# A new written-out order for the attention layer, and the second layer's gate summed by VectorE and DMA instead of TensorE

## The chip, the cores and the metric

One core of a Trainium2 chip runs the whole program. The metric is device time in microseconds (us) of one execution. The names of engines are those of the profile: PE is TensorE (PEld its weight loads), DVE is VectorE, ACT is ScalarE, POOL is GpSimd, SP is SyncE, which issues the big loads. Times inside the profiled execution are counted from its first instruction.

## The reference

A decoder trunk of two layers over 256 tokens of width 1024, batch 1, all in float32. Cut to what matters:

```python
for i in range(2):
    shift, scale, gate = split(c @ ada_w[i] + ada_b[i], 3)      # each of width 1024
    h = rmsnorm(x, norm_g[i]) * (1 + scale) + shift
    y = nsa_mixer(h, ...) if i == 0 else mlstm_mixer(h, ...)
    x = x + gate * y
return rmsnorm(x, final_g)
```

Layer 0 is sparse attention with three branches: keys and values compressed by a small network (`gelu(flat @ w1 + b1) @ w2 + b2`), selected blocks, and a sliding window. With 256 tokens the last two see all keys that the causal mask leaves. Layer 1 is a chunkwise mLSTM with 8 heads. Both multiply the mixer's output by a SiLU gate path and project it with `w_out`. The `gate` of each layer is a product of the vector `c` (1024) with a 1024x1024 part of `ada_w`.

## The kernel before

**Numbers.** A weight arrives as a float32 tile (`raw`, 128x1024, 512 KB). ACT rounds it into `wh` (L169, the step `hi`), DVE writes the rest into `wl` (L174, `lo`), and every product is three matmuls: `wh` with the high part of the activations, `wl` with it, `wh` with the low part. There are 10 `raw` buffers and 6 pairs of `wh` and `wl`.

**The loads.** One list of loads is issued by SP in its order (L86). A load is issued when the buffer that it takes over is free, so SP stands still behind a load that has no buffer.

**Layer 0** (`first_phase`, `nsa`, `attention`) runs under a manual schedule: each engine executes its instructions exactly as the program writes them. `first_phase` multiplies the first weights as they arrive. From then on the string `ORDER` sets the order of all engines and of the loads. Its words are steps:

- `k:kk,part` multiplies part of the key and value weights of one 128-row block; `hi` and `lo` make the next weight's halves. A `hi` also appends the next weight to the list of loads.
- `hidden:n` (L584) multiplies two loads of the compressing network's first weight, four in all. `gelu:0..2` (L669 to L676) is its activation, spread over DVE, ACT (`Square` L670, `Tanh` L674) and DVE (L676). `turned` (L681) is the first matmul behind it.
- `S:n,a` scores, `m` minima, `e` exponentials, `f` factors, `T` transposes on PE (L830), `t` their copies, for eight pairs of heads `n` and two halves of the tokens.
- `sXY:n,j` scales the probabilities by the factors (L825), branch 0 on engine X and branch 1 on engine Y, where p, v and a stand for POOL, DVE and ACT. Each letter is two instructions, called a pair here.
- `z:n,q` are steps of the gate path's products (twelve matmuls 128x256 each), `d` columns of layer 1's scale and shift (DVE, L873).
- `gp:k` loads one block of layer 0's gate weight and scales it by `c` on ACT (L652). `ga:k` adds it to the tile `gate0` with an adding DMA that POOL issues (L889). Before it POOL copies one column of `gate0` (L888, `seen`), which waits until the adding DMA before has landed. POOL executes in order, so all that stands behind `seen` waits too.

**Layer 1** (`layer2`) is ordered by the framework's scheduler, engine by engine. Loops run over 8 heads (`head`), four pairs of wide products (`og_unit`, `z_post`) and 16 blocks of the output weight (`project`, `finish`). Its gate (`gate_sums`, twice, for 512 columns each) multiplies the gate weights by `c` in eight DVE instructions (L1050), splits the sum into two float32r parts (ACT L1053, DVE L1054), sums over partitions with two matmuls against ones (L1057), which also spread the sum over all partitions, and copies the result into `gate1` (ACT, L1058). POOL multiplies a quarter of each output weight by `gate1` (L165). The half with columns 512 to 1023 comes first.

Of the kernel before, what the change touches and what calls it, by code (L numbers as in the profile page):

```python
# [23 lines left out]
class Kernel:  # L24
# [605 lines left out]
    ckeys cscores:1 cscores:0 ccopy:1 cvalues:0 sap:1,0 T:1,0,1 t:1,0,1 S:2,0 spp:1,1 d:0,2 S:2,1 zo:0 T:0,1,1 gp:4 cvalues:1 lo d:0,3 T:0,1,0 t:0,1,1  # L630
    m:2,0 m:2,1 z:1,0 ccopy:0 ctokens:0 t:0,1,0 cdist:0 ctokens:1 cdist:1 e:2,0 e:2,1 T:1,0,0 t:1,0,0 z:1,1 d:1,0 T:1,1,1 t:1,1,1 S:3,0 hi z:1,2 gp:5
    S:3,1 T:1,1,0 lo t:1,1,0 f:2 cexp m:3,0 V:0 V:1 cprobs ga:4 spp:2,0 T:2,0,0 m:3,1 z:1,3 e:3,0 T:2,0,1 S:4,0 hi cparts:0 S:4,1 t:2,0,0 cparts:1
    zt:1 spv:2,1 zo:1 t:2,0,1 cturned:0 lo e:3,1 f:3 T:2,1,0 T:2,1,1 t:2,1,0 ga:5 t:2,1,1 z:2,0 z:2,1 m:4,0 m:4,1 S:5,0 cpt:0 e:4,0 z:2,2 sap:3,0
    T:3,0,1 T:3,0,0 spv:3,1 C:0 z:2,3 d:1,1 e:4,1 d:1,2 t:3,0,1 t:3,0,0 S:5,1 f:4 y:0 T:3,1,1 lo hi gp:6 T:3,1,0 t:3,1,0 m:5,0 svp:4,0 V:2 t:3,1,1 V:3
    T:4,0,0 ga:6 spa:4,1 m:5,1 T:4,0,1 S:6,0 zt:2 e:5,0 e:5,1 t:4,0,1 t:4,0,0 cturned:1 lo S:6,1 zo:2 z:3,0 d:1,3 d:2,0 T:4,1,1 C:1 T:4,1,0 f:5 hi
    z:3,1 z:3,2 hi t:4,1,1 m:6,0 y:1 gp:7 spv:5,0 T:5,0,1 t:4,1,0 m:6,1 d:2,1 e:6,0 svp:5,1 t:5,0,1 lo z:3,3 cpt:1 Y:0 T:5,0,0 lo t:5,0,0 e:6,1 f:6
    V:4 T:5,1,1 ga:7 T:5,1,0 S:7,0 C:2 t:5,1,0 m:7,0 t:5,1,1 spa:6,1 zt:3 S:7,1 m:7,1 zo:3 spa:6,0 d:2,2 d:2,3 d:3,0 V:5 out:0 d:3,1 T:6,0,1 e:7,1
    e:7,0 f:7 gs T:6,1,0 gc g4 Y:1 t:6,0,1 out:1 t:6,1,0 T:6,0,0 T:6,1,1 params d:3,2 l:1,1,2 l:0,1,2 l:1,0,2 y:2 hi hi t:6,1,1 t:6,0,0 lo saa:7,1
    T:7,1,0 sap:7,0 T:7,0,1 t:7,0,1 t:7,1,0 l:0,0,2 l:0,1,3 hi T:7,1,1 t:7,1,1 T:7,0,0 t:7,0,0 d:3,3 lo lo Y:2 hi nh:0 hi lo V:6 V:7 C:3 l:0,0,3 y:3
    l:0,0,4 nl:0 l:0,1,4 l:0,1,5 l:0,0,5 Y:3 l:0,0,6 lo nh:3 nl:3 l:0,0,7 l:0,1,6 l:0,1,7 root l:1,1,3 l:1,0,3 l:1,1,4 g5 r:0,0 l:1,0,4 l:1,0,5 sq:0,0  # L640
    l:1,0,6 r:0,1 nh:2 sq:0,1 nl:2 sc:0 x:0,1 nh:1 x:0,0 l:1,0,7 tr:0,0 nh:4 nl:1 rp:1,0 tr:0,1 md:0,1 l:1,1,5 md:0,0 ro:0,0 re:0,0 l:1,1,6 ro:0,1
# [605 lines left out]
    def layer2(self):  # L1247
        nc, t, pc, p2, ident = self.nc, self.t, self.pc, self.p2, self.ident
        pcb = self.pcb
        g = nc.gpsimd  # L1250
# [300 lines left out]
        self.gate1 = self.T(pc, [P, D], tag="gate")  # L1551
        ones = self.T(p2, [P, P], F32R)
        bias = self.T(p2, [P, D])
        g.memset(ones.bitcast(F32), 1.0)
        g.memset(bias, 0.0)
        nc.gpsimd.dma_start(bias[0:1], t["ada_b"][1:2, 2048:3072])
# [113 lines left out]
```

## Time and profile before

| what | value |
|---|---|
| time of three runs | 419.70, 420.06, 420.30 us; median 420.06 |
| time of the profiled execution | 419.18 us |
| its span, first to last instruction | 417.4 us |
| PE busy | 406.9 us (97%) |
| DVE, ACT, POOL busy | 342.8, 282.8, 93.7 us |
| granted TensorE clock, mean | 0.998 of full speed |

The difference between the profiled time and its span, 1.8 us, lies around the program. A busy PE is not PE without loss: matmuls overlap, so a short wait shows in the distance between their starts rather than in the busy time.

### The profile page before, as it was taken

The numbers are of one execution on the slowest core, as the hardware profiler recorded it, in microseconds if no ns is written. First come the engines' busy times: TensorE is split into PE (matmuls) and PEld (weight loads), VectorE is DVE, ScalarE is ACT, GpSimd is POOL, SyncE is SP. The second block draws the span as 40 slices with busy tenths as digits, with TensorE's granted clock in tenths as the row PEclk, the third lists the DMA queues.
The fourth block names the chain that finished last, engine by engine and source line by source line (L and its number), as shares of the span: only waits on it lengthen the run. The fifth ranks groups of instructions, "written<-read, shape, count | busy, mean of one in ns | idle before, by whom it ended". The sixth has DMA issues, their size and how long they took to land.

```text
span 417.4 us, 7543 instructions
## 1 busy us (share of the span) xinstructions
PE 406.9 (97%) x2641; PEld 356.5 (85%) x2641; DVE 342.8 (82%) x716; ACT 282.8 (68%) x558; POOL 93.7 (22%) x163
## 2 busy tenths in 40 slices
PE   8999999989999999999999999999999999999994
PEld 5899998679889788888998999888888888888884
DVE  6999898979999999878782798899859996557553
ACT  6766687899999997767549866557446554564523
POOL 4000132256664420152324100000001241320000
PEclk9999999999999999999999999999999999999999
DMA  8999999999788988258684676378455776630002
GB/s 318 409 408 406 400 378 367 323 360 365 214 265 267 337 287 316 87 164 292 218 302 156 204 216 233 110 251 254 149 199 203 233 254 219 195 108 2 0 1 102
DMA packets 28616, 99.89 MB, mean 239 GB/s; under 512 B 3685, under 2 KB 3793, under 8 KB 28449
## 3 DMA queue, kind: packets, MB, share of 16 engines
q1 hardware_dynamic: 26208, 92.30, 62.3%
q0 software_dynamic: 2224, 6.83, 6.9%
q8 instruction: 21, 0.34, 0.3%
q10 hardware_dynamic: 144, 0.26, 0.2%
q14 instruction: 19, 0.15, 0.1%
HBM read 94.61 MB, written 1.10 MB: 229 GB/s over the span
## 4 chain that ended last, share of the span: by engine, by line
PE 90%; DMA 5%; ACT 2%; DVE 1%; SPq 1%; issue 0%; DVEq 0%; ACTq 0%
PE bank L549 10%; PE bank L550 10%; PE bank L551 10%; PE bank L439 8%; PE bank L1586 6%; PE bank L1584 6%; PE bank L1585 6%; PE bank L912 5%; PE bank L1497 5%; PE bank L1068 5%; PE bank L1179 4%; PE bank L847 3%; PE bank L830 3%; DMA raw<-in_start 2%; DMA raw<-in_path 2%; PE bank L1377 2%
## 5 line engine op out<-in xcount | busy, mean ns | idle before, releaser
L174 DVE TENSOR_TENSOR wl<-raw,wh 128x1024 fp32r<-128x1024 f32 (+4 forms) x119 | 138.2, 1175 | 36.1 <-ACT wh L169 35.2
L169 ACT ACTIVATE wh<-raw 128x1024 fp32r<-128x1024 f32 (+4 forms) x119 | 118.2, 1008 | 70.6 <-PE bank L551 31.8
L549 PE MATMUL bank<-wh,one 128*128 128x512 f32 (+2 forms) x208 | 77.1, 371 | 0.0
L550 PE MATMUL bank<-wl,one 128*128 128x512 f32 (+2 forms) x208 | 76.4, 367 | 0.0
L551 PE MATMUL bank<-wh,one 128*128 128x512 f32 (+2 forms) x208 | 76.2, 367 | 0.0
L1584 PE MATMUL bank<-one,wh 128*128 128x256 f32 x208 | 59.6, 286 | 0.0
L1586 PE MATMUL bank<-one,wl 128*128 128x256 f32 x208 | 59.0, 284 | 0.1
L1585 PE MATMUL bank<-one,wh 128*128 128x256 f32 x208 | 58.9, 283 | 0.0
L549 PEld LDWEIGHTS bank<-wh,one 128*128 128x128 f32 x208 | 39.2, 189 | 6.6 <-issue 0.4
L551 PEld LDWEIGHTS bank<-wh,one 128*128 128x128 f32 x208 | 39.2, 189 | 6.2
L550 PEld LDWEIGHTS bank<-wl,one 128*128 128x128 f32 x208 | 39.3, 189 | 5.9
L1586 PEld LDWEIGHTS bank<-one,wl 128*128 128x128 f32 x208 | 39.8, 192 | 0.3 <-DVE wl L174 0.3
L1584 PEld LDWEIGHTS bank<-one,wh 128*128 128x128 f32 x208 | 39.8, 192 | 0.2
L1585 PEld LDWEIGHTS bank<-one,wh 128*128 128x128 f32 x208 | 39.9, 192 | 0.2
L825 POOL TENSOR_SCALAR Pr<-Pr,f 128x128 f32<-128x128 f32 (+1 forms) x34 | 31.3, 941 | 27.1 <-DVE f L816 14.4
L439 PE MATMUL bank<-one,wh 128*128 128x256 f32 x224 | 29.8, 284 | 0.6 <-ACT one L413 0.4
L439 PEld LDWEIGHTS bank<-one,wh 128*128 128x128 f32 x224 | 28.1, 192 | 1.1 <-ACT one L413 0.6
L808 ACT ACTIVATE Pr<-Pr,mn 128x128 f32<-128x128 f32 (+1 forms) x64 | 28.2, 451 | 0.0
L165 POOL TENSOR_TENSOR raw<-raw,gate 128x256 f32<-128x256 f32 x16 | 16.4, 1035 | 47.0 <-DMA raw<-in_out_b 23.7
L1358 DVE SCALAR_TENSOR_TENSOR conv<-bank,one,conv 128x255 f32<-128x255 f32 (+2 forms) x48 | 20.1, 470 | 2.2 <-ACT conv L1353 2.2
L873 DVE CUSTOM_DVE_ANT_0 raw<-raw,one,one 128x1024 f32<-128x1024 f32 x16 | 20.6, 1311 | 0.0
L801 DVE CUSTOM_DVE_ANT_0 Pr<-bank,one 128x128 f32<-128x128 f32 (+1 forms) x64 | 18.7, 352 | 0.0
(343 smaller groups left out, 807.9 us busy)
## 6 DMA issues: line engine op xcount, KB each, us to landing
raw<-in_wide SPq DMA_DIRECT2D x44, 512.0 KB, 4.3
raw<-in_units SPq DMA_DIRECT2D x18, 512.0 KB, 4.7
raw<-in_turn SPq DMA_DIRECT2D x16, 512.0 KB, 6.1
raw<-in_out_b SPq DMA_DIRECT2D x16, 512.0 KB, 4.0
raw<-in_start SPq DMA_DIRECT2D x8, 512.0 KB, 9.8
Q<-in_columns SPq DMA_DIRECT2D x8, 512.0 KB, 9.6
raw<-in_gate SPq DMA_DIRECT2D x8, 512.0 KB, 7.8
raw<-in_path SPq DMA_DIRECT2D x8, 512.0 KB, 8.5
```

The source lines that it names most:

```text
L169: self.nc.scalar.activation(v(hi), src, AF.Copy)
L174: (g or self.nc.vector).tensor_tensor(v(lo), src, v(hi).bitcast(F32), op=OP.subtract)
L439: nc.tensor.matmul(out, w[:, ch * P : ch * P + P], h[:, kk], start=(kk == 0 and m == 0 and ch % 2 == 0), stop=(kk == 7 and m == 2), skip_g ...
L549: nc.tensor.matmul(out, self.hh[:, kk, sl], wh, start=first, stop=False, skip_group_check=True)
L550: nc.tensor.matmul(out, self.hh[:, kk, sl], wl, start=False, stop=False, skip_group_check=True)
L551: nc.tensor.matmul(out, self.hl[:, kk, sl], wh, start=False, stop=last, skip_group_check=True)
L808: nc.scalar.activation(v, v, AF.Exp, bias=mn[:, a, br, j : j + 1], scale=-1.0, accum_out=sm[:, a, br, j : j + 1])
L825: es[br].tensor_scalar(v, v, f, None, op0=OP.mult)
L912: nc.tensor.matmul(out, l[:, sl], w[:, c0:c1], start=(k == 0 and m == 0), stop=(k == 7 and m == 2), skip_group_check=True)
L1584: nc.tensor.matmul(out, wh, self.hh[:, kk], start=first, stop=False, skip_group_check=skip)
L1585: nc.tensor.matmul(out, wh, self.hl[:, kk], start=False, stop=False, skip_group_check=skip)
L1586: nc.tensor.matmul(out, wl, self.hh[:, kk], start=False, stop=last, skip_group_check=skip)
```

## The change

Two things. The string `ORDER` is written anew as a whole, with the same steps but for the engines of some scalings; the loads follow it. In the second layer `gate_sums` no longer uses PE: DVE transposes the 128x512 sum in 32x32 blocks, sums the 32 values of each row, transposes again, and the four quarters of the partitions are joined over scratch in DRAM (`quarters`, then `whole`), read back as `four`, summed once more by DVE, and spread over 128 partitions by a DMA. Four DMAs of a half are issued by POOL and pinned in program order; each waits for the one ahead. The half of columns 512 to 1023 is now written ahead of head 4, the other one ahead of the third pair of wide products, and the eight loads of the gate weights move up in the list by one pair each.

```diff
     ORDER = """
-    hi k:0,0 k:0,1 hi lo lo hi k:0,2 k:1,0 lo gp:0 ga:0 k:1,2 k:2,0 k:1,1 hi k:2,2 k:3,0 k:4,0 qa:3 lo d:0,0 E:0,0 k:2,1 k:3,1 E:1,0 hi lo E:1,1 k:3,2
...
+    gp:0 hi lo k:0,0 k:0,1 k:0,2 hi k:1,0 k:1,1 k:1,2 k:2,2 lo k:3,2 hi hi lo k:4,2 hi lo lo k:2,1 E:1,0 k:3,1 k:2,0 k:4,1 E:0,0 hi lo k:5,2 k:6,2
...
         for n in range(4):
-            if n >= 2:
-                self.gate_stream(3 - n)
+            if n in (1, 2):
+                self.gate_stream(2 - n)
             pair(3 + n)
...
-    def gate_sums(self, n, bias, ones, out, bi):
+    def gate_sums(self, n, bias, out):
...
-        parts = [self.T(self.p2, [P, 512], F32R, tag="conv", bufs=2) for _ in range(2)]
-        nc.scalar.activation(parts[0], acc, AF.Copy)
-        nc.vector.tensor_sub(parts[1], acc, parts[0].bitcast(F32))
-        bank = self.bank(bi)
-        for m, w in enumerate(parts):
-            nc.tensor.matmul(bank, ones, w, start=(m == 0), stop=(m == 1))
-        nc.scalar.activation(out[:, 512 * n : 512 * n + 512], bank, AF.Copy)
+        turned = self.T(p2, [P, 512], tag="conv", bufs=2)
+        nc.vector.transpose(turned, acc)
+        sums, rows = [self.T(p2, [P, 32]) for _ in range(2)]
+        g.memset(sums, 0.0)
+        nc.vector.tensor_reduce(sums[:, 0:16], turned.rearrange("p (j r) -> p j r", r=32), axis=AX.X, op=OP.add)
+        nc.vector.transpose(rows, sums)
+        pin = self.tc.keep_in_program_order
+        parts = self.pd.tile([P, 32], F32, name=self.nm("quarters"), tag="quarters%d" % n)
+        whole = self.pd.tile([16, 32], F32, name=self.nm("whole"), tag="half%d" % n)
+        four, one = self.T(p2, [16, 4, 32]), self.T(p2, [16, 32])
+        pin(g.dma_start(parts, rows))
+        pin(g.dma_start(four, parts.rearrange("(i j) c -> j i c", i=4)[0:16]))
+        nc.vector.tensor_reduce(one, four.rearrange("j i c -> j c i"), axis=AX.X, op=OP.add)
+        pin(g.dma_start(whole, one))
+        pin(g.dma_start(out[:, 512 * n : 512 * n + 512], whole.rearrange("j c -> (j c)").unsqueeze(0).partition_broadcast(P)))
...
         for n in range(2):
+            if n:
+                self.gate_sums(1, bias, self.gate1)
             head(4 * n)
...
         for n in range(2, 4):
-            self.gate_sums(3 - n, bias, ones, self.gate1, 6)
+            if n == 2:
+                self.gate_sums(0, bias, self.gate1)
             bs = wide_bs()
```

The loads that SP issues around the four `hidden` steps, before (`in_hidden` are the compressing network's weights, `in_gate` layer 0's gate weight, `in_path` the gate path's, `in_turn` columns):

```order
L86 DMA raw_734<-in_path 128x1024
L86 DMA raw_784<-in_hidden 128x1024
L86 DMA raw_837<-in_hidden 128x1024
...
L86 DMA raw_935<-in_gate 128x1024
L86 DMA raw_958<-in_path 128x1024
L86 DMA raw_961<-in_path 128x1024
L86 DMA raw_1018<-in_hidden 128x1024
L86 DMA raw_1020<-in_hidden 128x1024
L86 DMA raw_1033<-in_turn 128x1024
```

And the same places of SP's list now:

```order
L86 DMA raw_734<-in_hidden 128x1024
L86 DMA raw_784<-in_hidden 128x1024
...
L86 DMA raw_902<-in_gate 128x1024
L86 DMA raw_905<-in_path 128x1024
L86 DMA raw_939<-in_hidden 128x1024
L86 DMA raw_996<-in_hidden 128x1024
L86 DMA raw_1006<-in_hidden 128x1024
L86 DMA raw_1008<-in_hidden 128x1024
L86 DMA raw_1030<-in_path 128x1024
```

The last two `in_hidden` loads, which `hidden:3` reads, stand one place further up, and the `in_path` loads are spread among the others.

ACT between the first exponentials and the `Tanh` of the compressing network (L674), before (`raw_1062` is a load of the gate path's weight, `one_160` a copy of values, `raw_1035` a block of the gate weight):

```order
L808 ACTIVATE Pr_1105,sm_1076<-Pr_1105,mn_1075 128x256 x2
L808 ACTIVATE Pr_1106,sm_1076<-Pr_1106,mn_1075 128x256 x2
L670 ACTIVATE y_228_1135<-y_227_1134 128x256
L652 ACTIVATE raw_1035<-raw_1035,one_8_72 128x1024
L169 ACTIVATE wh_1162<-raw_1062 128x1024
L619 ACTIVATE one_160_810<-bank_826 128x512
L674 ACTIVATE y_228_1135<-y_228_1135 128x256
```

And now:

```order
L169 ACTIVATE wh_1103<-raw_1030 128x1024
L808 ACTIVATE Pr_1106,sm_1090<-Pr_1106,mn_1089 128x128 x2
L808 ACTIVATE Pr_1107,sm_1090<-Pr_1107,mn_1089 128x128 x2
L670 ACTIVATE y_223_1117<-y_222_1116 128x256
L808 ACTIVATE Pr_1106,sm_1090<-Pr_1106,mn_1089 128x256 x2
L808 ACTIVATE Pr_1107,sm_1090<-Pr_1107,mn_1089 128x256 x2
L674 ACTIVATE y_223_1117<-y_223_1117 128x256
L652 ACTIVATE raw_1071<-raw_1071,one_8_72 128x1024
```

No load stands between the two functions any more: the weight `wh` is made ahead of the exponentials, and the gate's block behind `Tanh`.

POOL at the first scalings (L825), before; L888 is the copy that waits for the adding DMA before, L889 the next adding DMA, and L698 to L312 are memsets:

```order
L825 TENSOR_SCALAR Pr_1105<-Pr_1105,f_1145 128x128
L825 TENSOR_SCALAR Pr_1105<-Pr_1105,f_1145 128x256
L825 TENSOR_SCALAR Pr_1106<-Pr_1106,f_1145 128x128
L825 TENSOR_SCALAR Pr_1106<-Pr_1106,f_1145 128x256
L698 MEMSET one_251_1275 128x128
L699 MEMSET y_252_1276 128x256
L311 MEMSET one_25_103 128x8
L312 MEMSET one_27_104 128x8
L888 COPY seen_1309<-gate_813 128x1
L889 DMA gate_813<-raw_1035 128x1024
```

And now:

```order
L825 TENSOR_SCALAR Pr_1106<-Pr_1106,f_1163 128x128
L825 TENSOR_SCALAR Pr_1106<-Pr_1106,f_1163 128x256
L888 COPY seen_1225<-gate_813 128x1
L889 DMA gate_813<-raw_1071 128x1024
L698 MEMSET one_251_1257 128x128
L699 MEMSET y_252_1258 128x256
L311 MEMSET one_25_103 128x8
L312 MEMSET one_27_104 128x8
L825 TENSOR_SCALAR Pr_1107<-Pr_1107,f_1163 128x128
L825 TENSOR_SCALAR Pr_1107<-Pr_1107,f_1163 128x256
...
L825 TENSOR_SCALAR Pr_1189<-Pr_1189,f_1341 128x128
```

Half of the first pair of heads (`Pr_1107`, both branches) is now scaled by POOL alone, behind an adding DMA. In the whole layer POOL has 19 pairs of scalings where it had 17, and three halves more (0,1, 3,1 and 4,1) whose two branches are both its own.

## Rows read from the trace of the kernel before

**Rows 1.** The page: busy time of each engine, with its share of the span and its instructions.

```profile
PE 406.9 (97%) x2641; PEld 356.5 (85%) x2641; DVE 342.8 (82%) x716; ACT 282.8 (68%) x558; POOL 93.7 (22%) x163
```

**Rows 2.** Stretches of the span: us, busy time of each engine (with instructions), granted clock, busy share of the DMA engines, GB/s.

```profile
core 0: us, PE busy (x) PEld busy (x) DVE busy (x) ACT busy (x) POOL busy (x), PEclk, DMA share, GB/s
66.00:71.00 5.00, 5.00 (x44) 4.18 (x44) 3.67 (x5) 4.36 (x7) 1.11 (x2) 1.00 1.04 397
71.00:78.00 7.00, 6.18 (x44) 3.46 (x42) 6.44 (x22) 6.97 (x18) 3.29 (x6) 1.00 1.02 312
78.00:87.00 9.00, 7.73 (x60) 6.60 (x57) 6.07 (x23) 6.51 (x18) 4.01 (x9) 1.00 1.03 320
...
100.00:120.00 20.00, 20.00 (x168) 18.27 (x167) 19.59 (x68) 19.42 (x61) 9.42 (x14) 1.00 0.84 262
120.00:140.00 20.00, 20.00 (x174) 17.24 (x173) 19.86 (x75) 19.68 (x61) 12.43 (x15) 1.00 0.90 262
```

**Rows 3.** The timeline of PE from 68 to 87 us: start, length, engine, line, operation, tiles, count, and in brackets idle time ahead of it and what ended it.

```profile
68.98 5.40 PE L584 MATMUL bank<-raw,Pr 128*64 128x256 f32 x48
...
74.90 0.40 PE L782 MATMUL bank<-KH,Q 128*128 128x512 f32 x1
...
75.69 0.50 PE L782 MATMUL bank<-KH,Q 128*128 128x512 f32 x1 [0.15 <-DVE Q L578]
...
76.44 0.65 PE L584 MATMUL bank<-raw,Pr 128*64 128x256 f32 x2
...
77.73 1.94 PE L584 MATMUL bank<-raw,Pr 128*64 128x256 f32 x14 [0.65 <-DMA raw<-in_hidden]
...
79.61 0.38 PE L549 MATMUL bank<-wh,one 128*128 128x256 f32 x1
...
84.69 0.49 PE L830 MATMUL bank<-one,Pr 128*128 128x128 f32 x3
86.45 0.41 PE L681 MATMUL bank<-one,y 128*128 128x128 f32 x2 [1.27 <-DVE y L676]
```

**Rows 4.** The timelines of ACT and DVE just ahead of that last wait.

```profile
84.00 1.06 ACT L169 ACTIVATE wh<-raw 128x1024 fp32r<-128x1024 f32 x1 [2.02 <-DMA raw<-in_path]
...
85.44 0.41 ACT L674 ACTIVATE y<-y 128x256 f32<-128x256 f32 x1
...
85.88 0.43 DVE L676 SCALAR_TENSOR_TENSOR y<-y,y 128x256 f32<-128x256 f32 x1 [2.41 <-ACT y L674]
```

**Rows 5.** Loads and adding DMAs: the timelines of SP and POOL, SP's own waits (us in total, times, longest), an issue group (KB each, us to landing), and the landing times of the seven adding DMAs (L889).

```profile
64.81 1.46 SPq L86 DMA_DIRECT2D raw<-in_path  x2
70.95 1.50 SPq L86 DMA_DIRECT2D raw<-in_hidden  x2
74.41 5.30 SPq L86 DMA_DIRECT2D raw<-in_path  x3
...
68.28 0.91 POOL L889 DMA_DIRECT2D gate<-raw  x1 [5.28 <-ACT raw L652]
76.16 0.87 POOL L889 DMA_DIRECT2D gate<-raw  x1 [0.35 <-POOL seen L888]
...
SPq L86 <- PE bank L584: 4.8, 2, 4.7
...
raw<-in_hidden SPq DMA_DIRECT2D x8, 512.0 KB, 6.1
...
DMA to landing us min/median/max: 5.2/7.2/9.9
```

**Rows 6.** The timeline of POOL at three of its scalings.

```profile
82.12 3.26 POOL L825 TENSOR_SCALAR Pr<-Pr,f 128x128 f32<-128x128 f32 x4 [5.09 <-ACT raw L652]
...
119.38 2.33 POOL L825 TENSOR_SCALAR Pr<-Pr,f 128x128 f32<-128x128 f32 x2 [2.89 <-DVE f L816]
...
122.77 2.90 POOL L825 TENSOR_SCALAR Pr<-Pr,f 128x128 f32<-128x128 f32 x2
```

**Rows 7.** What the gate's sum costs: the chain that ended last (start, us, what), and the DVE groups (busy, mean ns of one, idle ahead).

```profile
16.92 32.72 PE bank L439 x270
319.33 0.48 PE bank L1057 x2
360.43 0.48 PE bank L1057 x2
...
L1050 DVE SCALAR_TENSOR_TENSOR adaA<-raw,one,adaA 128x512 f32<-128x512 f32 x14 | 10.4, 746 | 0.7 <-DMA raw<-in_gates 0.6
L1054 DVE TENSOR_TENSOR conv<-adaA,conv 128x512 fp32r<-128x512 f32 x2 | 1.4, 682 | 0.0
L740 DVE TENSOR_REDUCE one<-tz 128x32 f32<-128x512 f32 x1 | 0.7, 677 | 0.0
L1313 DVE STREAM_TRANSPOSE one<-one 128x32 f32<-128x32 f32 x1 | 0.2, 197 | 0.0
```

**Rows 8.** How far the second layer's operands are ahead of PE: a stretch as in rows 2, the page's group of ACT's weight halves, and DVE and PE at head 4.

```profile
280.00:300.00 20.00, 20.00 (x109) 17.38 (x108) 18.41 (x51) 9.75 (x21) 0.00 (x0) 1.00 0.67 211
...
L169 ACT ACTIVATE wh<-raw 128x1024 fp32r<-128x1024 f32 (+4 forms) x119 | 118.2, 1008 | 70.6 <-PE bank L551 31.8
...
294.44 0.55 DVE L1372 TENSOR_TENSOR pl<-DT,ph 128x384 fp32r<-128x384 f32 x1
...
298.28 0.40 PE L1377 MATMUL bank<-V,pl 128*128 128x258 f32 x2
```

**Rows 9.** Small DMAs of POOL (KB each, us to landing), and POOL's first multiplications by the gate in the second layer.

```profile
whole<-adaA POOLq DMA_DIRECT2D x1, 4.0 KB, 4.1
...
gate<-whole POOLq DMA_DIRECT2D x1, 512.0 KB, 6.9
...
321.49 4.20 POOL L165 TENSOR_TENSOR raw<-raw,gate 128x256 f32<-128x256 f32 x4 [11.74 <-ACT gate L1058]
```

More of the change, by code (lines that the diff above doesn't have):

```diff
@@ L625 @@
     ORDER = """
-    hi k:0,0 k:0,1 hi lo lo hi k:0,2 k:1,0 lo gp:0 ga:0 k:1,2 k:2,0 k:1,1 hi k:2,2 k:3,0 k:4,0 qa:3 lo d:0,0 E:0,0 k:2,1 k:3,1 E:1,0 hi lo E:1,1 k:3,2
-    hi k:4,2 hi lo lo k:5,2 E:0,1 k:5,0 k:6,0 k:7,0 qb:3 k:4,1 k:6,2 k:7,2 hidden:0 hidden:1 qa:0 gp:1 ga:1 qa:1 qb:1 qa:2 kd qb:0 qb:2 G:0 hidden:2
-    S:0,0 S:0,1 G:1 vo:1 gp:2 ga:2 vo:0 hi hi m:0,0 hidden:3 e:0,0 m:0,1 e:0,1 lo gelu:0 d:0,1 k:5,1 f:0 k:6,1 k:7,1 gp:3 hi S:1,0 S:1,1 vo:2 gelu:1
-    spa:0,0 z:0,0 T:0,0,0 m:1,0 e:1,0 gelu:2 spv:0,1 m:1,1 turned t:0,0,0 e:1,1 z:0,1 z:0,2 lo lo second hi hi z:0,3 zt:0 T:0,0,1 f:1 ga:3 t:0,0,1
@@ L630 @@
[L630 to L641, printed above, removed]
@@ L642 @@
-    l:1,1,7 r:1,1 n:0,0 v:0,0 re:0,1 sq:1,0 sq:1,1 sc:1 x:1,1 n:0,1 n:0,2 nl:4 v:0,1 v:1,0 nh:5 x:1,0 v:1,1 tr:1,0 tr:1,1 md:1,1 v:2,0 md:1,0 v:2,1
-    ro:1,0 re:1,0 ro:1,1 gt:0 re:1,1 nl:5 v:0,2 v:1,2 n:1,0 n:1,1 n:1,2 gt:1
+    gp:0 hi lo k:0,0 k:0,1 k:0,2 hi k:1,0 k:1,1 k:1,2 k:2,2 lo k:3,2 hi hi lo k:4,2 hi lo lo k:2,1 E:1,0 k:3,1 k:2,0 k:4,1 E:0,0 hi lo k:5,2 k:6,2
+    k:3,0 k:4,0 k:5,0 k:6,0 k:7,0 qa:1 qa:3 qb:3 d:0,0 qb:1 hidden:0 gp:1 E:1,1 hi E:0,1 ga:0 hidden:1 ga:1 gp:2 qa:2 qb:2 k:7,2 kd qa:0 k:5,1 G:0
@@ new lines @@
+    qb:0 G:1 vo:0 hi lo hidden:2 lo S:0,0 hidden:3 hi m:0,0 e:0,0 gelu:0 S:0,1 m:0,1 e:0,1 gelu:1 lo z:0,0 gp:3 S:1,0 ga:2 f:0 vo:1 gelu:2 z:0,1
+    sap:0,0 S:1,1 m:1,0 k:6,1 d:0,1 k:7,1 hi ga:3 turned z:0,2 vo:2 second m:1,1 T:0,0,1 T:0,0,0 z:0,3 spp:0,1 e:1,0 ckeys e:1,1 t:0,0,0 cvalues:0
+    S:2,0 t:0,0,1 cscores:0 lo cscores:1 f:1 spa:1,0 cvalues:1 params d:0,2 zt:0 T:1,0,1 S:2,1 ccopy:0 ccopy:1 ctokens:0 T:0,1,0 t:1,0,1 zo:0 d:0,3 hi
+    gp:4 T:0,1,1 t:0,1,1 t:0,1,0 hi z:1,0 z:1,1 ctokens:1 T:1,0,0 m:2,0 e:2,0 t:1,0,0 z:1,2 cdist:0 z:1,3 lo d:1,0 m:2,1 e:2,1 zt:1 cdist:1 cexp ga:4
@@ new lines @@
+    spp:1,1 f:2 spp:2,0 S:3,0 zo:1 T:1,1,1 T:1,1,0 gp:5 m:3,0 t:1,1,0 S:3,1 m:3,1 V:0 cprobs t:1,1,1 d:1,1 e:3,0 hi hi cparts:1 cparts:0 V:1 svp:2,1
+    S:4,0 S:4,1 T:2,0,0 T:2,0,1 t:2,0,1 t:2,0,0 e:3,1 z:2,0 cturned:0 lo T:2,1,1 T:2,1,0 lo ga:5 z:2,1 t:2,1,1 cpt:0 z:2,2 t:2,1,0 cturned:1 f:3
+    spa:3,0 C:0 m:4,0 T:3,0,1 T:3,0,0 m:4,1 z:2,3 e:4,0 e:4,1 t:3,0,0 y:0 V:2 d:1,2 f:4 spp:3,1 T:3,1,0 lo S:5,0 S:5,1 gp:6 ga:6 t:3,0,1 t:3,1,0 hi
+    T:3,1,1 t:3,1,1 d:1,3 m:5,0 e:5,0 svp:4,0 zt:2 m:5,1 e:5,1 zo:2 V:3 T:4,0,0 t:4,0,0 T:4,0,1 S:6,0 C:1 S:6,1 y:1 z:3,0 spp:4,1 d:2,0 T:4,1,0
@@ new lines @@
+    t:4,0,1 f:5 cpt:1 spv:5,0 T:4,1,1 z:3,1 z:3,2 m:6,0 spv:5,1 m:6,1 t:4,1,0 hi gp:7 t:4,1,1 e:6,0 ga:7 hi lo d:2,1 T:5,0,0 z:3,3 T:5,0,1 V:4 lo C:2
+    t:5,0,0 t:5,0,1 S:7,0 T:5,1,1 T:5,1,0 lo Y:0 e:6,1 t:5,1,0 f:6 S:7,1 m:7,0 m:7,1 t:5,1,1 spa:6,0 zt:3 zo:3 Y:1 sap:6,1 hi V:5 out:0 T:6,0,1 d:2,2
+    d:2,3 T:6,1,0 gs out:1 l:1,1,2 d:3,0 e:7,0 e:7,1 f:7 lo l:1,0,2 y:2 t:6,0,1 t:6,1,0 gc d:3,1 T:6,1,1 T:6,0,0 l:0,0,2 d:3,2 l:0,0,3 g4 g5 saa:7,1
+    sva:7,0 t:6,0,0 t:6,1,1 hi d:3,3 T:7,1,0 T:7,0,1 lo t:7,1,0 t:7,0,1 hi lo l:0,1,2 T:7,0,0 t:7,0,0 T:7,1,1 t:7,1,1 V:6 V:7 C:3 Y:2 l:0,0,4 l:0,1,3
@@ new lines @@
+    y:3 hi l:0,1,4 lo Y:3 hi l:0,1,5 l:0,0,5 l:0,0,6 lo l:0,0,7 l:0,1,6 l:0,1,7 l:1,0,3 nh:3 nl:3 r:0,0 l:1,1,3 l:1,0,4 l:1,1,4 root l:1,0,5 r:0,1
+    nh:0 nh:1 sq:0,0 sq:0,1 nl:0 sc:0 x:0,1 nl:1 l:1,0,6 l:1,0,7 rp:1,0 nh:4 x:0,0 tr:0,0 nh:2 md:0,0 tr:0,1 md:0,1 ro:0,1 l:1,1,5 l:1,1,6 l:1,1,7
+    ro:0,0 sq:1,0 nl:2 n:0,0 n:0,1 r:1,1 sq:1,1 re:0,0 re:0,1 sc:1 x:1,1 nh:5 nl:4 v:0,0 v:0,1 v:1,0 v:1,1 n:0,2 x:1,0 tr:1,0 md:1,0 tr:1,1 md:1,1
+    v:2,0 v:2,1 ro:1,0 re:1,0 ro:1,1 re:1,1 nl:5 v:0,2 v:1,2 n:1,0 n:1,1 n:1,2 gt:0 gt:1
@@ L1042, in gate_stream @@
             self.add(None, [P, 2, 512], self.t["gates"][4 * n + j])
-    def gate_sums(self, n, bias, ones, out, bi):
-        nc = self.nc
+    def gate_sums(self, n, bias, out):
+        nc, p2 = self.nc, self.p2
+        g = nc.gpsimd
         acc, src = self.T(self.pc, [P, 512], tag="adaA", bufs=2), bias[:, 512 * n : 512 * n + 512]
@@ L1446, in layer2 @@
         ys = {}
+        self.gate1 = self.T(pc, [P, D], tag="gate")
+        bias = self.T(p2, [P, D])
+        g.memset(bias, 0.0)
+        nc.gpsimd.dma_start(bias[0:1], t["ada_b"][1:2, 2048:3072])
         for n in range(2):
+            if n:
+                self.gate_sums(1, bias, self.gate1)
             head(4 * n)
@@ L1549, in finish @@
                 nc.sync.dma_start(o[:, 512:], xo[:, 1, 512:])
[L1551 to L1556, printed above, removed]
         for n in range(2, 4):
-            self.gate_sums(3 - n, bias, ones, self.gate1, 6)
+            if n == 2:
+                self.gate_sums(0, bias, self.gate1)
             bs = wide_bs()
```

## The prediction

> **What bounds the kernel now.** The busy times come first: PE works 406.9 of 417.4 us, so only two things can shorten the run, fewer matmuls or fewer waits of PE [rows 1]. The stretches then show where it waits. From 100 to 140 us PE is busy throughout, with DVE and ACT at 97 to 99% beside it; from 71 to 87 it is not, and in the same stretch the DMA engines are full (share 1.02 and 1.03), while DVE and ACT have spare time [rows 2]. The second layer has a full PE: 280 to 300 us is an example [rows 8].
>
> The timeline of PE names the waits of the bad stretch [rows 3]. I count lost time by starts. Four matmuls of 128x512 stand between 74.90 and 76.44. A pair of such matmuls is 0.48 on the chain [rows 7], so they need 0.96 and took 1.54: 0.58 lost, most of it for Q from DVE and the rest for a load. `hidden:3` starts at 76.44 and its successor at 79.61, 3.17 us; the three `hidden` steps from 68.98 are 5.40, 1.80 each: 1.37 lost, waiting for its second load. `turned` starts at 86.45. The three transposes before it start at 84.69 and are 0.49 long by a modelled end; the idle time behind them is 1.27. Together 3.2 us.
>
> The two big waits have their causes one view further. `hidden:3` needs the two loads issued at 70.95. SP had stood 4.7 us on them because their buffers were those of `hidden:0`, and an adding DMA issued at 68.28 shared the engines [rows 5]. `turned` waited for DVE's L676, which waited 2.41 for ACT's `Tanh`, which stood behind a weight half that waited 2.02 for a load [rows 4]. That load was issued at 74.41, just ahead of the adding DMA of 76.16; adding DMAs take 5.2 to 9.9 us to land [rows 5].
>
> **The change part by part.**
>
> *The gate's sum.* PE loses two pairs of matmuls, each 0.48 on the chain [rows 7]: 0.96 us, with nothing put in their place on PE. This is the surest term. DVE pays for it. A half loses one subtraction (0.68) and gains a reduction over 512 values (0.68), a transpose of 128x32 (0.20), a small reduction and a transpose of 128x512 [rows 7]. The trace has no such transpose: at least the 0.20 of the small one, at most sixteen of them, 3.15; I take 0.70, as the other operations on 128x512 cost. The small reduction lies between 0.20 and 0.68; I take 0.25. So about 1.15 more per half, between 0.6 and 4.0. What hides it: ACT's weight halves spent 31.8 us waiting for PE to release a buffer, so weights are as far ahead as six buffers allow, and head 4's last operand is ready at 294.99 where PE asks at 298.28 [rows 8], 3.3 us. At the upper bound this cover would be gone and a head would cost up to 0.7 per half; at 1.15 nothing. The eight multiplications (0.746 each) also move: by the order the first half's move from among heads 0 to 3 to ahead of them, the second half's into the space between heads 3 and 4. DVE's 18.41 of 20 in that stretch [rows 8] loses about what it gains.
>
> The DMA chain of a half is four DMAs one behind the other on POOL. The nearest rows are 4.1 for a store of 4 KB and 6.9 for a spread of 512 KB [rows 9]; the chain is three of the first and one of the second, about 19 us. Its reader is L165, which so far waited 11.74 for the gate and ran at 321.49 [rows 9]. The first half's chain now starts some 20 us sooner, by the multiplications' new place; the second half's DMAs stand between POOL's L165s and can hold them for some 4 us each. POOL's wait of 11.74 shrinks by as much, so this costs nothing; with that cover gone it would be the whole of such a wait, 4 to 7.
>
> *The new order, at `hidden:3`.* Its loads stand one place further up: 512 KB at 397 GB/s [rows 2] is 1.3 us. They still take over the buffers of `hidden:0`, which now comes one `k` step of six matmuls 128x304 earlier, about 0.8 us (0.121 per 256 columns from 32.72/270 [rows 7]). Issued at about 70.1 and with the measured 6.1 to landing [rows 5], the second is there between 75.6 (the lag of 5.4 that the first one had before, an estimate from 70.95 and 76.44) and 76.4. PE without its waits would have asked at 75.9 before; now it has one `k` step more and one pair of 128x512 scores less ahead, 0.2 earlier. So of 1.37 about 0.5 stays (bounds 0 and 1.37). The Q wait stays as it is.
>
> *The new order, at `turned`.* PE's cover between `hidden:3` and `turned` was three `k` steps, two score steps, one `z` step and a turn, 79.61 to 85.0, 5.4 us. It is now three score steps, two `z` steps and two `k` steps: 0.96+0.48+0.96 for the scores, 2x1.45 for `z` and 2x0.73, all from 0.121 and 0.24 a matmul [rows 7], 6.8 us. The chain on the other side took 86.3-79.6 = 6.7, of which 2.02 was ACT standing at a load [rows 4]; that load is now taken ahead of the exponentials. 4.7 against 6.8: the wait of 1.27 goes, with 2 us to spare. What is late next there would be the `in_path` load itself, now issued behind `hidden:3`'s loads and so due at about 77.5, just when `hidden:3` ends.
>
> *The rest of the order* moves fillers (columns, gate blocks, scalings). I take off 0.3, the size of the Q wait, for one new small wait.
>
> Sum: 0.96 + (1.37-0.5) + 1.27 - 0.3, and 0.2 of load wait ahead of `hidden:3`, is 3.0. Against the profiled time, 419.18, that is 416.2. The profiled execution lies 0.9 below the median of the three runs; on that median, 420.06, the prediction is 417.0.
>
> **The rivals.**
>
> *A. Given back behind 87 us.* PE arrives 2 us earlier in a stretch where DVE idles 0.41 and 0.14 of 20, and ACT 0.58 and 0.32 [rows 2]. If their work is not ahead by as much, PE waits for operands until it is late again, and only about 0.5 of the order's gain is left: 420.06-0.96-0.5 = 418.6. For it: these shares. Against it: DVE idled 2.93 us in 78 to 87 [rows 2], 2.41 of it on the same `Tanh` [rows 4], so it gains with PE.
>
> *B. The order does not do what it is for.* The DMA engines are full from 66 to 87 and the bytes are the same; if the adding DMA of block 1, whose block now arrives earlier, moves ahead of `hidden:3`'s loads and costs them their place, `hidden:3` and `turned` wait as before. Then the gate alone is left, less a small wait: 419.4.
>
> *C. Slower: POOL late at the turns.* Three halves more have both branches scaled on POOL. Four scalings cost 3.26 when undisturbed, but two of them cost 2.33 and 2.90 elsewhere [rows 6]: stretched, four are up to 5.8. The first of the three stands behind `seen`, which waits for an adding DMA issued at about 76, landing at 81 to 86 [rows 5]; with 1.2 for the next one's issue, 0.9 of memsets and 3.26 it is done between 87 and 91.5, stretched 94. PE asks for it at about 93 by the steps ahead of it. If each of the three comes late by 1.3, 4.0 in sum, the gain is gone and it decides; at 5.8 each with no slack, 3 x 1.7 = 5.1 late, the time is 420.06-3.0+5.1 = 422.2. Against it: one wait of POOL for `seen` in the profile already lies in idle time.
> The Trainium skill's GPSIMD Engine Reference, section Specifications, says that GpSimd's SBUF interfaces are shared with VectorE and contend with DVE instructions that read two SBUF inputs; DVE's weight rests are of that kind, and by that rule every pair moved to POOL also costs both sides. The stretched pairs of rows 6 agree with it. By the rows' undisturbed pair the move is free, by the rule it is case C.
>
> **How the numbers follow.** The forecast, gains of 2 to 4.8, has 0.56; its top is all 3.2 of waits, 0.96, and 0.6 for small waits elsewhere. A has 0.18, B 0.14, C 0.12. What this measurement can tell from no change is about 0.2%, 0.84 us: faster than 419.2 are the forecast and A, 0.74; within it B, 0.14; slower C, 0.12. The range runs from 415.4, the forecast's top, to 419.8, which takes in A and B and leaves out C and a little else.
>
> **What would show it.** Right: no L1057 on PE; `hidden:3` at 2.3 us or less; no wait of L681 above 0.3; the stretch from the first wide product to the end 0.96 shorter; PE full from 100 to 140. Wrong: L681 or L584 idle as before (B), idle PE at L830 behind POOL's L825 (C) or at matmuls that wait for ACT and DVE between 87 and 145 (A), or any PE wait near heads 4 to 7, which would say that DVE's gate work was not covered.

## The result, and the profile after

The changed kernel takes **416.86 us** (median of six runs, 416.44 to 417.84) where the kernel before, timed beside it, takes 420.18: a ratio of 0.992, with a 95% interval of 0.9904 to 0.9936. It was timed again later and gave 417.13 us, 0.9935 (0.9919 to 0.995). Its profiled execution took 416.44 us, with a span of 414.7; the profiled one before had 417.4.

The first view is the page's busy times; they stand beside [rows 1].

```profile
PE 406.3 (98%) x2637; PEld 355.7 (86%) x2637; DVE 342.5 (83%) x720; ACT 279.4 (67%) x552; POOL 99.2 (24%) x176
```

Four matmuls are gone, and PE is idle for 8.4 us where it was for 10.5. Where that came from is seen in the same stretches as in [rows 2]; the last row, and the one of before in the fence behind it, run from the same matmul of the second layer's first wide product (L1188 now, L1179 before) to the end of the span.

```profile
71.00:78.00 7.00, 7.00 (x57) 4.63 (x54) 5.87 (x15) 3.61 (x8) 2.50 (x5) 1.00 1.00 327
78.00:87.00 9.00, 9.00 (x70) 8.64 (x70) 7.87 (x32) 9.00 (x28) 3.06 (x6) 1.00 1.03 360
120.00:140.00 20.00, 19.98 (x159) 16.98 (x158) 19.62 (x75) 19.56 (x58) 13.29 (x17) 1.00 0.86 250
...
180.59:414.70 234.11, 228.53 (x1288) 200.46 (x1288) 177.31 (x320) 135.39 (x218) 36.63 (x55) 0.99 0.55 181
```

```profile
182.26:417.40 235.14, 229.56 (x1292) 201.24 (x1292) 177.68 (x314) 137.39 (x222) 35.64 (x47) 1.00 0.54 178
```

From 71 to 87 us PE is now full, with the DMA engines as full as before. The second layer is 1.03 us shorter, all of it PE's busy time. The same matmul starts at 182.26 before and at 180.59 now, so the first layer gained 1.67. The timeline of PE shows how, beside [rows 3].

```profile
75.99 1.95 PE L584 MATMUL bank<-raw,Pr 128*64 128x256 f32 x16
77.87 0.50 PE L782 MATMUL bank<-KH,Q 128*128 128x512 f32 x1
...
84.62 0.38 PE L681 MATMUL bank<-one,y 128*128 128x128 f32 x2
...
89.77 1.93 PE L720 MATMUL bank<-Q,one 128*32 128x256 f32 x32
91.93 0.84 PE L830 MATMUL bank<-one,Pr 128*128 128x128 f32 x3 [0.23 <-ACT Pr L652]
```

`hidden:3` takes 1.88 us from start to start where it took 3.17, and `turned` has no idle time ahead of it. The new order stands in seven profiled executions, this one and six of the runs below: in six of them `hidden:3` takes 1.88, in one 2.60. In exchange there is a new wait at 91.93. The timelines of ACT and DVE show the step that was moved; [rows 4] has it before.

```profile
77.89 1.06 ACT L169 ACTIVATE wh<-raw 128x1024 fp32r<-128x1024 f32 x1 [3.33 <-DMA raw<-in_path]
...
82.68 0.40 ACT L674 ACTIVATE y<-y 128x256 f32<-128x256 f32 x1
83.34 0.42 DVE L676 SCALAR_TENSOR_TENSOR y<-y,y 128x256 f32<-128x256 f32 x1
```

ACT still stands at a load, for even longer (3.33 us), but ahead of the exponentials, where nobody on PE waits for it: the first turns, which need the exponentials and of which one stood ahead of `turned` before, now all stand behind it.

### The profile page after: what moved, and what is told of

It is laid out like the page before. It is cut to its first block, busy times and chain, and to the rows that moved or that the text cites. A ratio compares the mean times of both kernels' runs of the same rounds, so it can differ in the third digit from the quotient of the medians.

```text
span 414.7 us, 7569 instructions
## 1 busy us (share of the span) xinstructions
PE 406.3 (98%) x2637; PEld 355.7 (86%) x2637; DVE 342.5 (83%) x720; ACT 279.4 (67%) x552; POOL 99.2 (24%) x176
## 4 chain that ended last, share of the span: by engine, by line
PE 87%; DMA 6%; DVE 3%; ACT 2%; issue 1%; SPq 0%; DVEq 0%; ACTq 0%
PE bank L551 10%; PE bank L549 10%; PE bank L550 10%; PE bank L439 7%; PE bank L1596 6%; PE bank L912 5%; PE bank L1595 5%; PE bank L1594 5%; PE bank L1512 5%; PE bank L1077 5%; PE bank L1188 4%; PE bank L847 3%; PE bank L830 3%; DMA Q<-in_columns 3%; PE bank L1386 2%; DMA raw<-in_opening 2%
## 5 line engine op out<-in xcount | busy, mean ns | idle before, releaser
L174 DVE TENSOR_TENSOR wl<-raw,wh 128x1024 fp32r<-128x1024 f32 (+3 forms) x119 | 138.2, 1176 | 36.0 <-ACT wh L169 35.5
L825 POOL TENSOR_SCALAR Pr<-Pr,f 128x128 f32<-128x128 f32 (+1 forms) x38 | 33.1, 985 | 20.4 <-DVE f L816 13.5
L165 POOL TENSOR_TENSOR raw<-raw,gate 128x256 f32<-128x256 f32 x16 | 13.2, 822 | 53.8 <-DMA raw<-in_out_b 49.3
```

The source lines that it names most:

```text
L174: (g or self.nc.vector).tensor_tensor(v(lo), src, v(hi).bitcast(F32), op=OP.subtract)
L825: es[br].tensor_scalar(v, v, f, None, op0=OP.mult)
```

## Experiments

**The two halves apart.** The new gate with the old order, and the new order with the old gate.

> The old order with the new sum of the second layer's gate. Theory of the prediction: the four matmuls against ones leave PE (two pairs of 0.48 us) and the DVE work that replaces them is covered, so the run is 0.9 to 1.0 us shorter than before (ratio 0.9977), the first layer's waits stay where they were (hidden:3 3.2 us long, turned waiting 1.3 us), and PE has no wait in the second layer. Rival: DVE's new work comes out from under its cover at the heads, or the chain of DMAs makes the scaled output weights late; then PE waits in the second layer and the gain is below 0.5 us.

> The new order with the old sum of the second layer's gate. Theory: the first layer ends 1.6 to 2.1 us sooner, as the two traces differ at its end (1.64 us of PE's lost time), and the second layer takes what it took, so the ratio to before is 0.995 to 0.996. Rival: the measured ratio of both changes together, 0.992 or 3.3 us, holds more than the two traces show (2.7 us); if that is the order's, this run shows 2.4 us or more.

Gate alone: 419.06 us, ratio 0.9975 (0.996 to 0.9991), that is 1.05 us, as the theory had it. Order alone: 418.22, ratio 0.9945 (0.9927 to 0.9963), 2.3 us by the ratio and 1.9 by the medians, between the theory's 0.995 and the rival's 2.4 us; the interval takes in both. The two add up to 3.4 us by the ratios and 2.9 by the medians, and both together gave 3.3: within the intervals, about 1 us, nothing shows that they touch each other. The first run's profile keeps the old waits, one of them longer than in [rows 3]:

```profile
86.63 0.41 PE L681 MATMUL bank<-one,y 128*128 128x128 f32 x2 [2.02 <-DVE y L676]
```

So the same order of the first layer lost 1.27 us at `turned` in one execution and 2.02 in another.

**One step of the order alone: Tanh.**

```diff
-... gp:3 hi S:1,0 S:1,1 vo:2 gelu:1
+... gelu:1 gp:3 hi S:1,0 S:1,1 vo:2
```

> The old order with one word moved: the second step of the compressing network's activation goes ahead of the gate block and of the weight half that waits for a load, so ACT does Tanh right behind Square. Theory of the prediction: ACT standing at that load was the cause of the wait at turned (L681), so this wait falls from 1.27 us of idle to at most 0.2; the time falls by 1.0 to 1.4 us if nothing behind it is late. Rival A: the scalings and turns that stand behind the same weight half on ACT are late instead, PE waits at L830, and less than 0.5 us is left of the gain at the end of the first layer. Rival B: the wait at L681 stays, since something else on DVE or ACT is as late.

419.28 us, ratio 0.9971 (0.9958 to 0.9983). The timeline of PE:

```profile
85.29 0.38 PE L681 MATMUL bank<-one,y 128*128 128x128 f32 x2
92.12 1.24 PE L720 MATMUL bank<-Q,one 128*32 128x256 f32 x17 [0.93 <-ACT wh L169]
```

The wait at `turned` goes and a wait of 0.93 comes at `cscores` (L720), behind two weight halves on ACT. The cause I named for `turned` is right, and most of the gain is given back 7 us later in this profile, as rival A has it, but at L720 and not at L830. The runs gained 1.2 us by the ratio and 0.8 by the medians, more than the 0.3 (1.27 - 0.93) that the profile leaves; the 2.02 above is a possible reason, not a shown one.

**One step of the order alone: the loads of hidden:3.**

```diff
-... hi hi m:0,0 hidden:3
+... hi hidden:3 hi m:0,0
```

> The old order with one word moved: hidden:3 stands ahead of the second of the two weight halves before it, so that its two loads are one place further up in SP's list and one in_path load is behind them; PE's order is as before. Theory: its first load takes over a buffer that is free at 66, its second one that of the first load of hidden:0, free at 70.7; the second lands about 1.3 us sooner, near 76.4, and the idle time inside hidden:3 falls from 0.65 us to 0 to 0.3 (its length from 3.2 to 2.3 or less). But turned waits for ACT, which waits for a load that lands at 83.9 either way; so PE waits there as much longer, about 2.2 us, and the time is the same within 0.3 us. Rival, the plain sum of my prediction, in which the two waits are gained apart from each other: the time falls by 0.9 to 1.3 us.

421.2 us, ratio 1.0024 (1.0009 to 1.0039): slower, which neither theory had.

```profile
76.26 1.98 PE L584 MATMUL bank<-raw,Pr 128*64 128x256 f32 x16
83.90 0.33 PE L830 MATMUL bank<-one,Pr 128*128 128x128 f32 x1 [0.48 <-POOL Pr L825]
84.81 0.44 PE L830 MATMUL bank<-one,Pr 128*128 128x128 f32 x2 [0.58 <-POOL Pr L825]
87.14 0.66 PE L681 MATMUL bank<-one,y 128*128 128x128 f32 x2 [1.89 <-DVE y L676]
```

One place is enough to free `hidden:3`: its first load now finds a buffer at 66.28, so that only one load still waits for a buffer of `hidden:0`. But with full DMA engines a place is only exchanged: the `in_path` load that moved behind holds ACT 2.20 us ahead of the exponentials, so factors, POOL's scalings and the turns are late, and the load ahead of `Tanh` is as late as ever. What the 1.89 did beside is told below.

**The suspected competitor taken away.** The kernel before without two adding DMAs.

```diff
-            nc.gpsimd.dma_start(self.gate0, raw, accum_op=OP.add)
+            if k > 2:
+                nc.gpsimd.dma_start(self.gate0, raw, accum_op=OP.add)
```

> The kernel before with the adding DMAs of gate blocks 1 and 2 left out, those that were issued at 68.28 and 76.16 us (so layer 0's gate lacks two of its eight blocks; nothing else is left out). Theory: the loads of hidden:3 and the load that ACT stood at ahead of Tanh landed late because these two DMAs shared the engines with them; without them the loads land 1 to 2 us sooner, the idle time inside hidden:3 (0.65) and ahead of turned (1.27) goes, and the time falls by 1.5 to 2.7 us. Rival: the loads wait for their buffers and the engines are full of other loads anyway; then both waits stay within 0.4 us of what they were and the time falls by less than 0.5 us.

416.97 us, ratio 0.9926 (0.9905 to 0.9947): 3.1 us. Both waits are gone, and PE has none in the turns behind them:

```profile
77.59 1.95 PE L584 MATMUL bank<-raw,Pr 128*64 128x256 f32 x16
...
84.97 0.38 PE L681 MATMUL bank<-one,y 128*128 128x128 f32 x2
...
90.80 1.93 PE L720 MATMUL bank<-Q,one 128*32 128x256 f32 x32
92.67 0.55 PE L830 MATMUL bank<-one,Pr 128*128 128x128 f32 x3
```

So the adding DMAs were the root of both waits. The loads of `hidden:3` took (issue group of SP from 70 to 73 us, KB, us to landing; before, after, and without the adding DMAs):

```profile
raw<-in_hidden SPq DMA_DIRECT2D x2, 512.0 KB, 5.9
```

```profile
raw<-in_hidden SPq DMA_DIRECT2D x2, 512.0 KB, 4.8
```

```profile
raw<-in_hidden SPq DMA_DIRECT2D x2, 512.0 KB, 4.0
```

Before and without the adding DMAs these two loads are issued at the same distance from the start of `hidden:0`, 1.97 us (70.95 and 72.16), so the whole difference is in the landing: what the adding DMAs take of the engines. The load ahead of `Tanh` took 6.5 us to landing instead of 9.5 and was, counted in the same way, issued 1.3 sooner.

**The adding DMA only moved.** The old order with `gp:1 ga:1` ahead of `hidden:0`.

> The kernel before with the words gp:1 and ga:1 moved ahead of hidden:0, and nothing else: the gate block's load stands four places further up in SP's list, so its adding DMA is issued near 63 to 64 us instead of 68.28, as in the changed kernel, while the loads of hidden:3 keep their places and buffers' order. Theory: the adding DMA's share of the engines while hidden:3's loads are in flight was 1.1 us of their time to landing (4.4 and 5.2 us in the changed kernel, 5.4 and 6.3 before); with it out of the way the idle time inside hidden:3 (0.65) falls to 0 to 0.2, and turned then waits longer by what PE gains unless the in_path load ahead of Tanh lands sooner too. So hidden:3 is 2.2 us long or less and the time falls by 0.2 to 1.0 us. Rival: only the place of the loads counted (they were issued 0.9 us sooner in the changed kernel); then hidden:3 stays 2.8 us or longer and the time is the same within 0.2 us.

420.29 us, ratio 1.0001 (0.9983 to 1.0019). The adding DMA starts at 65.26 instead of 68.28, the two loads take 5.5, and both waits stay:

```profile
78.44 1.94 PE L584 MATMUL bank<-raw,Pr 128*64 128x256 f32 x14 [0.65 <-DMA raw<-in_hidden]
87.98 0.41 PE L681 MATMUL bank<-one,y 128*128 128x128 f32 x2 [2.10 <-DVE y L676]
```

This is the rival's outcome. To start that DMA sooner does not free `hidden:3`. It did not leave the engines to these loads either: the `in_path` load issued ahead of them now takes 8.8 us to landing instead of 6.8, and the next adding DMA starts at 74.46 instead of 76.16, while they are on their way. One place further up in SP's list did free `hidden:3`, in the run above.

**The Tanh step undone in the new order.** `gelu:1 gelu:2` behind the second `hi`, next to `turned`.

> The changed kernel with Tanh and what surrounds it put back behind a gate block and a weight half that waits for a load, as it stood before. Theory: hidden:3 keeps its full speed, but turned waits again for L676, by 2 to 2.6 us, so at that point PE has lost again all that it had won there and at hidden:3; behind 87 us the waits at L830 that PE's early arrival caused go (0.84 us), and the time rises by 1.2 to 2 us against the changed kernel. Rival: PE is held up by ACT and DVE behind 87 us in either case, so only what is left of the gain there, less than 0.6 us, is lost.

420.72 us, ratio to before 1.0018 (1.0 to 1.0035): 3.6 us slower than the changed kernel, more than both theories. The row of `turned`, and the stretches from there on:

```profile
88.41 0.69 PE L681 MATMUL bank<-one,y 128*128 128x128 f32 x2 [2.81 <-DVE y L676]
```

```profile
86.00:88.00 2.00, 0.00 (x0) 0.00 (x0) 1.49 (x5) 1.58 (x3) 1.70 (x3) 0.91 1.04 426
88.00:90.00 2.00, 1.59 (x8) 1.59 (x9) 1.22 (x5) 1.92 (x9) 2.00 (x7) 0.50 1.03 408
90.00:92.00 2.00, 2.00 (x12) 2.00 (x11) 1.20 (x8) 1.80 (x7) 2.00 (x3) 0.50 1.06 414
92.00:94.00 2.00, 2.00 (x11) 2.00 (x11) 0.62 (x3) 0.27 (x2) 0.19 (x1) 0.50 1.04 264
```

The wait is 2.81 us, and behind it the granted clock (the third number from the end) is 0.50, which is the 1.2 GHz level, until about 94: PE does 11 or 12 matmuls in 2 us instead of 20. The wait is paid, and then a good part of it once more: from `turned` to the matmul from which the second layer is counted above, this execution takes 97.8 us, and two of the unedited changed kernel 95.8 and 96.0.

**What was given back, and the scarce engine.** Four kernels on one chip: the changed kernel again, one that makes the late factors and scalings sooner (`d:0,2 cscores:1 f:1 lo`, `S:2,1 T:1,0,1` and `svp:4,0 m:5,0 ... d:1,3` in place of `lo cscores:1 f:1`, `T:1,0,1 S:2,1` and `d:1,3 m:5,0 e:5,0 svp:4,0`), one with more DVE work in the gate, and one with three scalings taken from POOL (`spv:0,1`, `spv:3,1`, `spa:4,1`).

> The changed kernel once more, unedited, beside the next three on the same chip, so that they can be compared with it. By its first timing: 0.992 of before, 416.9 us, with about 0.8 us of idle time of PE at L830 near 92 us, and 0.2 to 0.5 near 122.

> The changed kernel with two small moves in its order: near 88 us DVE makes the factors f:1 ahead of a weight rest (L174) and PE takes the scores S:2,1 ahead of the turn T:1,0,1; near 120 us DVE does its scaling of svp:4,0 ahead of a column and of the minima. Theory: what the new order gave back behind 87 us (0.84 us at L830 behind ACT's scaling, 0.24 to 0.5 at L830 behind DVE's) came from factors and scalings that stand on DVE behind one long instruction; both waits go and the time falls by 0.8 to 1.2 us below the changed kernel's. Rival A: DVE and ACT are full there, so PE waits a little later for something else and the time is the same within 0.3 us.

> The changed kernel with the 128x512 transpose of the second layer's gate done five times instead of once, four times for nothing: 2.8 us more of DVE work per half, 5.6 in all. Theory of the prediction: head 4 has 3.3 us of cover and a half with 4.0 us of extra work costs at most 0.7 us, so the time rises by 0 to 1.4 us, likely 0 to 0.7. Rival: there is no cover of that size, since the heads' own operands stand behind the transposes on DVE; then PE waits 2 to 2.8 us per half and the time rises by 4 to 5.6 us.

> The changed kernel with the three halves whose two branches are both POOL's given back as they were: the second branch of 0,1 and 3,1 to DVE, that of 4,1 to ACT. Rival C of the prediction (POOL late at the turns, and its scalings and DVE's weight rests stretching each other): PE's waits at L830 near 92 and 122 us fall, and the time falls by 0.5 to 1 us. Theory: POOL's scalings are ready in time and DVE and ACT are the scarce engines there, so giving them 2.6 us more work makes the run slower by 0.2 to 1 us.

The changed kernel 0.9935 of before; factors first 0.9937 (0.9923 to 0.995); more DVE work 0.9933 (0.9916 to 0.9949); POOL's scalings back 0.9949 (0.9934 to 0.9964), 417.97 us against 417.13.

Factors first is its rival A: the same time by the ratios. The waits at 92 and 122 go, and two others take their place:

```profile
93.70 0.88 PE L731 MATMUL bank<-one,y 128*128 128x128 f32 x4 [0.33 <-ACT y L652]
...
127.25 0.44 PE L830 MATMUL bank<-one,Pr 128*128 128x128 f32 x2 [0.44 <-POOL Pr L825]
```

The extra transposes were done, and the second layer, from the same matmul to the end, did not notice 4.7 us more of DVE time (182.04 against 177.31 above):

```profile
L1055 DVE STREAM_TRANSPOSE conv<-adaA 128x512 f32<-128x512 f32 x10 | 7.0, 704 | 0.0
```

```profile
181.96:416.10 234.14, 228.58 (x1288) 200.44 (x1288) 182.04 (x328) 135.62 (x218) 38.62 (x55) 1.00 0.54 181
```

With the scalings back on DVE and ACT the wait at L830 is 0.44, where the changed kernel has 0.23. But `hidden:3` waited for a load in this execution (2.60 us long) and PE came 0.9 later, and the run with more DVE work, whose first layer is that of the changed kernel, waits still longer there. The two rows, POOL's scalings back first:

```profile
93.29 0.84 PE L830 MATMUL bank<-one,Pr 128*128 128x128 f32 x3 [0.44 <-ACT Pr L652]
93.37 0.84 PE L830 MATMUL bank<-one,Pr 128*128 128x128 f32 x3 [0.56 <-ACT Pr L652]
```

DVE makes the factors (L816) at 92.57 and 92.64 in these two and at 91.21 in the changed kernel, so the profiles do not show what the scalings do to this wait. The times do so in part: rival C's gain of 0.5 to 1 us is refuted, and that POOL's share saves time (0.8 us by the medians) is only suggested, since the intervals overlap.

**The old order with three changes.** The new gate, `ga:1` early and `Tanh` first, nothing else.

> The old order with three of the changes on trial together and nothing else of the new order: the new sum of the second layer's gate, gp:1 and ga:1 ahead of hidden:0, and Tanh right behind Square. Theory, the sum of parts: 1.0 for the gate, up to 1.4 inside hidden:3, up to 1.4 at turned, less what comes back behind 87 us (1.1 us at the first cscores behind two weight halves in the run with Tanh alone; less here if the loads of those halves land sooner); so 416.4 to 418.0 us, a ratio of 0.991 to 0.995. If it is below the changed kernel's 0.992 the rest of the new order is worth nothing or costs time; the rival is that the rest of the new order carries the gain, and this version stays above 0.996.

418.64 us, ratio 0.9953 (0.9936 to 0.997), between the theory's 0.995 and the rival's 0.996. `hidden:3` still waits 0.62 and L720 waits 1.22 behind ACT: the rest of the new order is worth some 0.8 to 1.4 us by the two timings of the changed kernel, with intervals that touch or overlap. Of the versions that do all the work, none is faster than the changed kernel beyond its interval.

## Why the prediction was right, and where it was not

**The gate's sum** was right. PE's 0.96 measured 1.03 in the trace and 1.05 in the runs. The DVE durations in the changed kernel:

```profile
L1054 DVE STREAM_TRANSPOSE conv<-adaA 128x512 f32<-128x512 f32 x2 | 1.4, 703 | 0.0
L1057 DVE TENSOR_REDUCE one<-conv 128x16 f32<-128x512 f32 x2 | 1.3, 674 | 0.0
L1065 DVE TENSOR_REDUCE one<-one 16x32 f32<-16x128 f32 x2 | 0.7, 373 | 1.3 <-DMA one<-quarters 1.3
```

I took 0.70, 0.68 and 0.25; the small reduction was 0.12 longer. The upper bound, 0.7 us per half at 4.0 us more of DVE work, was too dark: 2.8 more per half on top of the real change cost nothing. I had read one head's lead as the whole cover, which is the likely reason and is not shown. The chain of four DMAs took some 16 us from the first issue at 275.98 to the last landing, where I had 19. POOL's first L165 came at 302 us and waited for ACT, not for the gate, and PE is full in the second layer as before.

**hidden:3** was the right mechanism with a mis-sized term. I said 0.5 of 1.37 would stay, with 6.1 to landing, the median of all eight such loads; the two of `hidden:3` took 5.9 before and 4.8 now, and next to nothing stayed (3.17 to 1.88 is 1.29). The step that failed is "Issued at about 70.1 and with the measured 6.1 to landing". The first of them was issued at 70.06, as said; but with one load fewer in front of them, which I had priced and then left out of the sum, and the adding DMA 5 us earlier (63.17), the two also landed sooner, the second at 75.7, which is the early end of my 75.6 to 76.4. The run that moved the adding DMA alone shows that this DMA's place is not enough, and the one with the loads one place up freed `hidden:3` by another buffer; which part of the new order shortens the landing, no run separates. The margin is small: `hidden:3` starts at 75.99, and in the execution where it took 2.60 the second load landed at 76.9.

**turned** was right: 1.27 expected, 1.27 gone, and the cause is shown by the run with `Tanh` alone (the wait goes) and the run that undoes it (2.81 comes back). The spare time was overestimated: the cover on PE was 6.75 us (77.87 to 84.62) where I had 6.8, but the chain to the end of L676 (83.76) took 5.9 instead of 4.7, so 0.9 was left and not 2. What was to be late next, the `in_path` load, came at 77.9 where I had 77.5, and holds ACT until then without harm.

**One new small wait, 0.3**, was the other mis-sized term. In PE's timeline three turns at 91.93 come 0.29 late against the run without adding DMAs (2.16 us behind L720's start instead of 1.87), and take 0.84 instead of 0.55; six turns from 121.89 on take 1.12 where the next six, from 126.17 on, take 0.82:

```profile
121.89 1.12 PE L830 MATMUL bank<-one,Pr 128*128 128x128 f32 x6
```

That is 0.9, three times my term. It is rival A's mechanism at less than half of A's size (A leaves 0.5 of the order's 2.6 and so takes back 2.1): PE comes sooner into a stretch where ACT and DVE have no slack, and the run with the factors first shows that to push one of them forward only moves the wait.

**The Q wait**, which I said would stay, shrank: the four matmuls of 128x512 now take 1.04 us (77.87 to 78.91) instead of 1.54. What I called 0.2 of load wait ahead of `hidden:3` gave about 0.1.

So the sum of 3.0 met the measured 3.3 (and 2.7 in the traces: 1.03 + 1.29 + 1.27 - 0.9) with two errors of 0.4 and 0.6 that lay on opposite sides. With the Q wait the parts come to some 0.6 more than the traces' 2.7, and where PE loses that again is not placed. That the totals lie so near each other is luck and says nothing for the terms.

**Rival B** was half true: the adding DMAs were the root, but the new order did get out of their way. **Rival C** had its mechanism and not its price. POOL and DVE do stretch each other. In the changed kernel, the timelines of DVE and POOL near 89 us:

```profile
88.84 2.02 DVE L174 TENSOR_TENSOR wl<-raw,wh 128x1024 fp32r<-128x1024 f32 x1
88.74 2.90 POOL L825 TENSOR_SCALAR Pr<-Pr,f 128x128 f32<-128x128 f32 x2
```

And DVE in the run with POOL's scalings back:

```profile
88.73 1.21 DVE L825 TENSOR_SCALAR Pr<-Pr,f 128x128 f32<-128x128 f32 x2
90.99 1.22 DVE L174 TENSOR_TENSOR wl<-raw,wh 128x1024 fp32r<-128x1024 f32 x1
```

With POOL out of the way the same weight rest takes 1.22, so the stretch costs DVE 0.8. But the two scalings cost DVE 1.21 when it does them itself, so the move to POOL costs it less than it frees. The Trainium skill's GPSIMD Engine Reference, section Specifications, says that GpSimd shares its SBUF interfaces with VectorE and contends with DVE instructions of two SBUF inputs; the trace agrees (2.02 against 1.22). By the runs it is no reason to leave the scalings on DVE here.

## What to carry to other kernels

With full DMA engines a load's place in the queue was not won in these runs, only exchanged: put the load that can be late in front of an engine whose work nobody waits for yet. A wait that was taken away where the other engines were full came back in part a few microseconds later, so price the arrival, not the wait. Work that left a full TensorE for engines with spare time brought its full price, with the new order and without it, as far as the intervals tell.
